# The first load of Q in a linear-attention kernel: one queue or two

## The chip, the cores and the metric

The kernel runs on one core of a Trainium2 chip. The metric is the time of one execution in microseconds on the device. A profiled execution gives in addition the span from the first to the last instruction and what every engine and DMA queue did inside it.

## The reference

For each of 8 x 12 heads, with Q, K and V of 512 rows by 64 in FP32:

```
Q_feat = np.maximum(0, Q) + 1
K_feat = np.maximum(0, K) + 1
KV = np.einsum('bhkd,bhkv->bhdv', K_feat, V)
K_sum = np.sum(K_feat, axis=2)
numerator = np.einsum('bhqd,bhdv->bhqv', Q_feat, KV)
denominator = np.einsum('bhqd,bhd->bhq', Q_feat, K_sum)
return (numerator / (denominator[:, :, :, None] + 1e-10)).astype(np.float32)
```

There is little arithmetic for each byte: 37.75 MB are read and 12.58 MB are written.

## The kernel before

The 96 heads are worked in 12 groups of 8 heads (`NG` is 12). Two neighbouring groups share their transfers: one load of K, one of V and one of Q, 1 MB each as it is written on chip, bring a pair of groups. These loads go by POOL's queue (`nc.gpsimd.dma_start`) and change FP32 to BF16 on the way, so each reads 2 MB from memory. The stores of all but the last two groups go by POOL's queue as well; the last ones go by SP's.

For one group, VectorE makes the features of K (`k_features`), VectorE and ScalarE copy V into a block layout (`v_blocks`: three copies of 32 partitions at L164 on VectorE, one at L162 on ScalarE), TensorE multiplies them (`keys_values`, L180), and ScalarE takes the result out of PSUM. VectorE makes the features of Q (`q_features`, L146), TensorE transposes them (L201), ScalarE copies the transposed tiles (L204), TensorE multiplies them by KV (`out_matmuls`, L214), and VectorE divides (`norms`, L231 and L232) into the tile that is stored.

The order of the work is written out by hand, under `tc.manual_schedule()`: each engine runs its instructions in the order of the program. The start matters here. The first pair of groups isn't loaded by three large loads: K and V come in two loads each, one per group, and Q comes in two halves of another kind. The first half is `q_first`, a tile of its own, loaded by `load_first_q` without a change of type, 128 rows of 8 KB, one for each partition; the second is loaded by `load_rest_q` on POOL's queue. In order of the program:

```
nc.gpsimd.memset(zero, 0.0)
q_first = load_first_q()
load("k", (0,))
load("v", (0,))
load_rest_q(q_first)
load("k", (1,))
load("v", (1,))
...
clear(0)
```

`clear` fills the block layout of V with zeros: VectorE takes five eighths (L249), ScalarE the rest (L250), then VectorE sets the columns of ones (L251). `q_first` is first read by `q_features(0)`, after the K features and V blocks of group 0.

Of the kernel before, what the change touches and what calls it, by code (L numbers as in the profile page):

```python
# [19 lines left out]
def kernel(  # L20
# [19 lines left out]
    nc = tc.nc  # L40

    B, H, S, D = Q.shape
    P = 128
# [10 lines left out]
    def view(t, c):  # L54
        return t.flatten_outer_dims().rearrange("(n p c) d -> p n c d", p=P, c=c)

    q_eights = view(Q, C4)
# [32 lines left out]

    def load_first_q():
        t = head_pool.tile([P, C4, D], FP32, name="q_first")
        nc.sync.dma_start(out=t, in_=q_eights[:, 0])
        return t

    def load_rest_q(t):
# [159 lines left out]
    with tc.manual_schedule():  # L256
# [4 lines that stand above are left out]
# [81 lines left out]
```

## Time and profile before

| | us |
|---|---|
| Time, median of 3 runs (lowest to highest) | 126.62 (126.32 to 127.39) |
| The profiled execution's own time | 126.47 |
| Its span, first to last instruction | 124.7 |
| VectorE busy | 90.1 |
| TensorE matmul busy | 64.2 |
| ScalarE busy | 59.6 |
| POOL busy | 26.1 |
| `q_first`: issue on SP, and from there to landing | 0.74, then 4.9 |

The busy times are inside the span. In the lines of the profile, PE is TensorE, DVE is VectorE, ACT is ScalarE, POOL is GpSimd and SP is SyncE. L93 and the like are lines of the kernel. In the slices, one digit is a fortieth of the span in tenths, so 9 is 90% or more. The DMA share is the time of the packets over the time of 16 DMA engines; packets overlap a little, so it can be above 1. The bytes are those written: a load that changes FP32 to BF16 counts half of what it reads. q0 is the queue that POOL feeds; q1 is a hardware queue, before the change that of SP. In a table of windows, the columns are the window, its length, the busy time and number of instructions of PE, PEld (weight loads), DVE, ACT and POOL, then the granted clock, the DMA share and GB/s.

### The profile page before, as it was taken

To read this page: it belongs to the slowest core of one execution; us is meant where nothing else is said; L and a number is where in the kernel's file an instruction comes from. 1 tells how busy PE (TensorE), PEld (TensorE's weight loads), DVE (VectorE), ACT (ScalarE), POOL (GpSimd) and SP (SyncE) were. 2 spreads that over 40 slices of the span, in tenths; PEclk is the share of its full clock that TensorE was granted. 3 is DMA by queue.
4 is the path that set the end of the run, shared out by engine and by line. 5 is a ranking of instruction groups with operands and counts; after the bars stand their busy time and mean duration, and the time that the engine had idled before them with its cause. 6 is when DMAs were issued, how large, how long until landed. Compare 5 with 4: busy or idle time off the path is not lost.

```text
span 124.7 us, 2349 instructions
## 1 busy us (share of the span) xinstructions
PE 64.2 (52%) x960; PEld 52.6 (42%) x960; DVE 90.1 (72%) x190; ACT 59.6 (48%) x86; POOL 26.1 (21%) x53
## 2 busy tenths in 40 slices
PE   0000874600596837939099690069394369874200
PEld 0000654600475826829088490058183158663000
DVE  4875735206999989998999950799958799969700
ACT  7505169806009981398803981603982283650000
POOL 6992020400001460207202070302020200020000
PEclk9999999995559996799855999657999855999655
DMA  3999999999999999999999999999999999999993
GB/s 89 320 212 216 206 211 212 212 215 218 206 212 212 220 213 206 212 215 217 230 406 327 210 212 219 212 342 395 230 202 215 219 247 417 419 417 415 406 409 135
DMA packets 11819, 32.13 MB, mean 258 GB/s; under 512 B 544, under 2 KB 544, under 8 KB 11680
## 3 DMA queue, kind: packets, MB, share of 16 engines
q0 software_dynamic: 10592, 28.84, 97.5%
q1 hardware_dynamic: 1216, 3.15, 6.7%
q8 instruction: 7, 0.11, 0.3%
q14 instruction: 4, 0.03, 0.1%
HBM read 37.75 MB, written 12.58 MB: 404 GB/s over the span
## 4 chain that ended last, share of the span: by engine, by line
DMA 51%; DVE 19%; PE 10%; ACT 7%; POOL 6%; issue 2%; DVEq 0%; ACTq 0%; POOLq 0%
DMA v_raw<-in_V_dram 51%; DVE o_sb L232 7%; PE kva_ps L180 7%; DVE v_all L164 7%; ACT qt L204 3%; ACT v_all L162 3%; POOL kva_all L271 2%; POOL k_raw L115 2%; DVE recip L231 2%; PE qt_ps L201 1%; PE o_ps L214 1%; POOL v_raw L115 1%; DVE qf L146 1%; DVE qt L204 1%; DVE kf L146 1%
## 5 line engine op out<-in xcount | busy, mean ns | idle before, releaser
L180 PE MATMUL kva_ps<-v_all,kf 128*64 128x260 bf16 x384 | 33.0, 343 | 16.8 <-DVE v_all L164 15.5
L214 PE MATMUL o_ps<-kva_all,qt 128*64 128x130 bf16 x384 | 19.7, 237 | 34.2 <-DVE recip L231 25.9
L164 DVE COPY v_all<-v_raw 32x2048 bf16<-32x2048 bf16 x36 | 26.1, 725 | 15.0 <-DMA v_raw<-in_V_dram 14.6
L180 PEld LDWEIGHTS <-kf 128*64 128x64 bf16 x384 | 26.6, 140 | 20.4 <-DVE v_all L164 15.9
L232 DVE TENSOR_TENSOR o_sb<-o_ps,recip 128x512 f32<-128x512 f32 x48 | 33.2, 692 | 1.6
L162 ACT COPY v_all<-v_raw 32x2048 bf16<-32x2048 bf16 x12 | 22.6, 1893 | 18.2 <-DMA v_raw<-in_V_dram 18.0
L214 PEld LDWEIGHTS <-qt 128*64 128x64 bf16 x384 | 13.7, 116 | 39.1 <-issue 23.2
L190 ACT CAST kva_all<-kva_ps 64x256 bf16<-64x256 f32 x24 | 8.9, 370 | 30.7 <-PE kva_ps L180 30.6
L204 ACT COPY qt<-qt_ps 128x1024 bf16<-128x1024 bf16 x23 | 22.2, 1015 | 2.2 <-PE qt_ps L201 1.7
L201 PE MATMUL qt_ps<-identity,qf 128*128 128x128 bf16 x192 | 14.8, 236 | 1.3 <-ACT qt L204 1.1
L135 POOL DMA_DIRECT2D out_dram<-o_sb x10 | 8.3, 830 | 32.1 <-DVE o_sb L232 27.3
L146 DVE TENSOR_SCALAR kf<-k_raw 128x1024 bf16<-128x1024 bf16 x24 | 9.5, 436 | 7.0 <-DMA k_raw<-in_K_dram 7.0
L201 PEld LDWEIGHTS <-qf 128*128 128x128 bf16 x192 | 12.6, 107 | 4.1 <-issue 1.8
L115 POOL DMA_DIRECT2D k_raw<-in_K_dram x7 | 5.4, 765 | 34.4 <-DVE kf L146 34.0
L231 DVE RECIPROCAL recip<-o_ps 128x8 f32<-128x8 f32 x48 | 9.6, 200 | 1.5 <-PE o_ps L214 1.2
L115 POOL DMA_DIRECT2D v_raw<-in_V_dram x7 | 5.4, 772 | 17.4 <-ACT v_all L162 17.4
L146 DVE TENSOR_SCALAR qf<-q_raw 128x1024 bf16<-128x1024 bf16 x22 | 8.2, 432 | 0.0
L249 DVE MEMSET v_all<- 128x2600 f32 x2 | 4.5, 2225 | 1.1 <-issue 1.1
L191 ACT CAST kva_all<-kva_ps 64x4 bf16<-64x4 f32 x24 | 4.1, 169 | 0.0
L121 POOL DMA_DIRECT2D q_raw<-in_Q_dram x5 | 3.5, 705 | 0.0
L250 ACT COPY v_all<-zero 128x1560 f32<-128x1560 f32 x2 | 2.9, 1488 | 0.0
L271 POOL MEMSET kva_all<- 128x130 bf16 x16 | 2.4, 196 | 0.0
(14 smaller groups left out, 6.6 us busy)
## 6 DMA issues: line engine op xcount, KB each, us to landing
out_dram<-o_sb POOLq DMA_DIRECT2D x10, 1024.0 KB, 25.2
k_raw<-in_K_dram POOLq DMA_DIRECT2D x5, 1024.0 KB, 21.7
v_raw<-in_V_dram POOLq DMA_DIRECT2D x5, 1024.0 KB, 21.8
q_raw<-in_Q_dram POOLq DMA_DIRECT2D x5, 1024.0 KB, 25.9
q_first<-in_Q_dram SPq DMA_DIRECT2D x1, 1024.0 KB, 4.9
k_raw<-in_K_dram POOLq DMA_DIRECT2D x2, 512.0 KB, 9.7
v_raw<-in_V_dram POOLq DMA_DIRECT2D x2, 512.0 KB, 11.4
out_dram<-o_sb SPq DMA_DIRECT2D x1, 1024.0 KB, 7.0
```

The lines of the kernel that those rows point to most:

```text
L115: nc.gpsimd.dma_start(out=bufs[x, s][:, ms], in_=drams[x][:, of])
L135: nc.gpsimd.dma_start(out=o_to[:, g % 2 : 2 * NP : 2], in_=outs[s][:, g % 2 : 2 * NP : 2])
L146: nc.vector.tensor_scalar(out=dst, in0=src, scalar1=1.0, scalar2=1.0, op0=ALU.add, op1=ALU.max)
L162: nc.scalar.copy(out=v_all[ps, g % 2, :, :, b * D : b * D + D], in_=v_raw[ps])
L164: nc.vector.tensor_copy(out=v_all[ps, g % 2, :, :, b * D : b * D + D], in_=v_raw[ps])
L180: nc.tensor.matmul(kva_ps[64 * n : 64 * n + 64], lhsT=kf[:, c, n, :], rhs=v_all[:, g % 2, n, c, :], start=(c == 0), stop=(c == C2 - 1),)
L190: nc.scalar.copy(out=kva[ps, :, n, 0:D], in_=kva_ps[ps, 0 : 4 * D].rearrange("p (b d) -> p b d", b=4))
L201: nc.tensor.transpose(qt_ps[:, c, r], qf[:, r, 2 * half + c, :, :], identity)
L204: copy(out=qts[g // 2][:, lo : lo + 2], in_=qt_ps.rearrange("p c r q -> p c q r"))
L214: nc.tensor.matmul(ops[c // 4][64 * j : 64 * j + 64, c // 2 % 2, (c % 2) * W : (c % 2) * W + W], lhsT=qt[:, c, q : q + 16, :], rhs=kva[:, ...
L231: nc.vector.reciprocal(out=recip, in_=cells[:, :, :, :, D:D1])
L232: nc.vector.tensor_tensor(out=o_sb[:, 2 * h + g % 2 : 2 * NP : NP, 4 * i : 4 * i + 4].rearrange("p n (b c) d -> p b c n d", b=2), in0=cell ...
```

## The change

The first load of Q is issued as two transfers of 64 partitions each. The first goes by SP's queue, the second by ScalarE's. Where they stand in the program, the tile that they fill and all that reads it stay.

```
     def load_first_q():
         t = head_pool.tile([P, C4, D], FP32, name="q_first")
-        nc.sync.dma_start(out=t, in_=q_eights[:, 0])
+        nc.sync.dma_start(out=t[0 : P // 2], in_=q_eights[0 : P // 2, 0])
+        nc.scalar.dma_start(out=t[P // 2 : P], in_=q_eights[P // 2 : P, 0])
         return t
```

## The prediction, made before the change was run

> **What bounds the kernel now.** I began with the page: the slices (part 2) and the chain that ended last (part 4).
>
> ```profile
> span 124.7 us, 2349 instructions
> PE 64.2 (52%) x960; PEld 52.6 (42%) x960; DVE 90.1 (72%) x190; ACT 59.6 (48%) x86; POOL 26.1 (21%) x53
> DMA  3999999999999999999999999999999999999993
> HBM read 37.75 MB, written 12.58 MB: 404 GB/s over the span
> DMA 51%; DVE 19%; PE 10%; ACT 7%; POOL 6%; issue 2%; DVEq 0%; ACTq 0%; POOLq 0%
> ```
>
> No compute engine is above 72%, but the 16 DMA engines are full in every slice except the first and the last. The kernel is one long transfer of 50.3 MB with the arithmetic beside it. So the end is set by the time at which the DMA engines begin, by how fast they work, and by nothing that a compute engine does inside the slack that it has. A microsecond of DMA-engine time lost anywhere comes out at the end.
>
> Next I read the table of half-microsecond windows over the start. Its last two columns are the DMA share and GB/s.
>
> ```profile
> 1.50:2.00 0.50, 0.00 (x0) 0.00 (x0) 0.13 (x1) 0.50 (x1) 0.50 (x1) 1.00 1.13 131
> 2.00:2.50 0.50, 0.00 (x0) 0.00 (x0) 0.50 (x1) 0.49 (x2) 0.50 (x2) 1.00 0.00 0
> 2.50:3.00 0.50, 0.00 (x0) 0.00 (x0) 0.50 (x1) 0.50 (x1) 0.50 (x2) 1.00 0.68 279
> 3.00:3.50 0.50, 0.00 (x0) 0.00 (x0) 0.50 (x1) 0.50 (x2) 0.50 (x2) 1.00 0.97 410
> 4.50:5.00 0.50, 0.00 (x0) 0.00 (x0) 0.11 (x1) 0.41 (x1) 0.50 (x2) 1.00 1.17 483
> 5.00:5.50 0.50, 0.00 (x0) 0.00 (x0) 0.50 (x1) 0.00 (x0) 0.43 (x3) 1.00 1.06 168
> ```
>
> Packets are booked in the window in which they start. Eight start just before 2 us (one for each of eight engines), none in the next window, and from about 2.6 us all engines work: up to 5 us over 400 GB/s are written, which is plain FP32, the first Q; from 5 us about 200 GB/s, which is a casting load (4 bytes read for 2 written). The DMA queues of three windows say whose packets these are. First 3.0 to 3.5, then 4.5 to 5.0, then 5.0 to 5.5:
>
> ```profile
> q1 hardware_dynamic: 25, 0.20, 96.5%
> ...
> q1 hardware_dynamic: 31, 0.24, 112.2%
> q0 software_dynamic: 2, 0.00, 4.3%
> ...
> q0 software_dynamic: 41, 0.08, 104.2%
> q1 hardware_dynamic: 14, 0.00, 1.6%
> ```
>
> q1 is the hardware queue (the first Q), q0 is POOL's. They do not mix: K(0), issued on POOL at 1.29, moves nothing until an engine has done its share of Q. Therefore the first Q's transfer is fully exposed. It is the head of the kernel's one resource, even though VectorE needs its data much later.
>
> The timeline of the start shows that slack.
>
> ```profile
> 0.74 0.39 SPq L93 DMA_DIRECT2D q_first<-in_Q_dram  x1
> 2.03 2.88 ACT L250 COPY v_all<-zero 128x1560 f32<-128x1560 f32 x2
> 10.89 1.89 ACT L162 COPY v_all<-v_raw 32x2048 bf16<-32x2048 bf16 x1 [5.97 <-DMA v_raw<-in_V_dram]
> 12.95 0.69 DVE L146 TENSOR_SCALAR qf<-q_first 128x1024 bf16<-128x1024 f32 x1
> ```
>
> **The change part by part.** The sum is against the profiled execution: 126.47 us, a span of 124.7 and 1.77 around it. It lies 0.15 under the median of 126.62, which the forecast leaves aside.
>
> Issue on ScalarE (added): one DMA instruction, 0.39 us by SP's row. Behind it in ScalarE's program stand the two zero-fills of L250 and then the V copy of L162. ScalarE is idle for 5.97 us before 10.89, so 0.39, or even the 1.28 us of a table load with it, is covered. Without that cover 0.39 would delay V's blocks, and so TensorE, at 12.98. There is one nearer reader: VectorE's L251 at 4.20 writes over what ScalarE clears. ScalarE's first fill ends near 3.5 (2.03 plus 1.49), so 0.7 us are free there, and VectorE has 1.74 us idle before 10.81 after that. Cost 0.
>
> Issue on SP (halved): SP has nothing else until 114.28. Cost 0.
>
> Waits: VectorE's first reading of Q at 12.95 now needs two arrivals. Q landed at 5.64 (0.74 plus 4.9). Even 3 us later it is 4 us early. A second semaphore is worth an issue gap, 0.02 to 0.04 us in the chain, and VectorE idles 0.87 us before 15.79: cost 0. At the end the program also waits for ScalarE's queue, long done: 0 to 0.04, taken 0.
>
> Transfer of Q: bytes and packets stay. From the 3.0 to 3.5 row a packet takes 0.965 x 16 x 0.5 / 25 = 0.309 us. There are 128 rows of 8 KB, so 8 packets or 2.47 us on each engine. What the change alters is that each half covers only 64 partitions. No transfer in this trace does that (all loads and stores cover 128), so I bound it. The lower bound is no loss: the 0.309 us stay, 4 and 4 packets. The upper bound is that half the partitions take half the rate, 0.618 us a packet, so the two halves, drained one after the other as q1 and q0 were, cost 4.94 in place of 2.47: plus 2.47 us. I choose between them by what the rows suggest about the 0.309. It is 26.5 GB/s for one engine, and hardly moves from window to window; stores and casting loads give 25 and 24 GB/s on their wider side (16 engines at 417 and at 2 x 212, over 16 and with their overlap). That is a fixed width somewhere, at the engine or at the memory it writes. If at the memory, sixteen engines on half of it share it two by two. The row nearest in kind is that of Q itself: a transfer that writes 4 bytes an element at that width, so nothing is spare to hide the sharing. I take sharing, with one correction: the engines do not start together. The rows show two batches, at 1.84 (0.74 of issue plus 1.1) and at 2.62, 0.78 apart for 64 rows each. With 32 rows in a batch I expect 0.39. For that long at each end of a half, one of a pair has the width alone: 4 packets then take 0.39 + (4 - 0.39/0.309) x 0.618 = 2.08 for the first, and as much from its own start for the other. Two halves are 4.16, a loss of 1.7 us.
>
> The Trainium skill speaks against the change here: "SBUF — State Buffer", in the sections "Door 1: The DMA port swizzle" and "Can I just issue two DMAs to hit both halves?", says that partitions 0 to 63 reach only 8 of 16 ports, gives 196 GB/s for a 1 MiB load to them against 328 to all, and says that two concurrent halves gain about 6% on one. By its 6% on 196 GB/s, 1.05 MB would take an estimated 5.0 us, a loss of 2.6; nothing in this trace shows such a port.
>
> Start of Q (moved): data flows from about 2.6, when the second batch of engines starts. If half the rows on each queue bring that forward to the first batch, 0.78 us is gained; that is the lower end, minus 0.78. Against it: the eight early packets start before 2.0, and yet nothing follows in 2.0 to 2.5, so early descriptors alone did not bring early data. The upper end is 0, or later for one half if ScalarE loads its table first, which costs nothing while SP's half or K keeps the engines busy. I take minus 0.2.
>
> The skill's page "DMA: Bandwidth & Descriptors", section "Queues, rings and completion order", has an engine take turns between queues packet by packet; the rows above show q1 done before q0 starts. By turns, a pair could step to opposite halves after one packet, and the loss would go towards 0.
>
> Order of arrival: V(0), which VectorE and ScalarE wait for at 10.8, stands behind K(0) in POOL's queue and behind all of Q on the engines, so it is late by the loss. What is late next is every load and store behind it. POOL issued loads 20 us ahead of their landing (21.7 us from issue to landing in the page), so no queue runs empty, and the shift reaches the end whole.
>
> Sum: 126.47 + 1.7 - 0.2 = 128.0 us.
>
> **The rivals.**
>
> First, no sharing: the width belongs to the engine, or an engine alternates halves. Then only the start counts: 126.47 - 0.2 = 126.3, down to 125.7 if the whole 0.78 is gained. For it: the fixed 0.309 could as well be the engine's, and the DMA share is already above 1 with 16 engines. Against: all those rows spread over all partitions. This is the case on the other side, not slower; it decides if a half's packet stays below about 0.34 us (8 x 0.03 is 0.2).
>
> Second, partial sharing: ScalarE's half comes after its table load (1.28 us), the engines are out of step, and some run K while their partner is on Q. Half of the loss is left: 126.47 + 0.85 - 0.2 = 127.1. For it: the table load stands at 0.74 in ScalarE's program now, and K is ready by then. Against: partners tend to meet again in the second half.
>
> Third, the split does not do what it says: the second half is drained strictly after the first, at full rate, or waits behind K and V. Q would land near 11 and still before 12.95: 126.5. I count it with the first.
>
> **How the numbers follow.** Sharing 0.52, partial 0.18, none (with the third) 0.30. The forecast is the likeliest, 128.0; its own range runs from 127.2 (more gained at the start) to 128.8 (126.47 + 2.47 less a little). A tenth of the cases lies above 128.7; the lowest tenth, a third of the no-loss case, lies below about 126.0. The range is 126.0 to 128.7. One per cent of the median, 1.27 us, is about what can be told from no change: sharing gives more than that in some eight of ten of its cases, partial in one of ten: slower 0.44. Faster by so much would need more than the 0.78 at the start: 0.04. Within 1%: 0.52.
>
> **What would show it.** Right: windows from 2.5 to 7 us with about 200 to 280 GB/s written by the hardware queues, packets near 0.6 us, K's first packet at 6.5 or later, V's landing 1.5 us after its 10.8, and the same tail shifted. Wrong: over 400 GB/s until 5 us (no sharing), K starting before 4.6 (a gain at the start), VectorE idle at 12.95 waiting for Q (the order broke), or a shift at 10.8 that is gone by 98.8, when the last V lands (the DMA was not the limit throughout).

## The result, and the profile after

The changed kernel takes 128.24 us (median of 6 runs, 127.87 to 128.74), against 126.59 (126.32 to 127.39, 6 runs) for the kernel before in the same comparison: a ratio of 1.0117, with an interval of 1.0093 to 1.0140. It is slower by 1.65 us. The profiled execution took 128.13 us, its span 126.4 (before: 126.47 and 124.7).

The page of the kernel after: the span, the DMA slices, the memory line, and the chain by engine.

```profile
span 126.4 us, 2351 instructions
...
DMA  3999999999999999999999999999999999999993
...
HBM read 37.75 MB, written 12.58 MB: 398 GB/s over the span
...
DMA 52%; DVE 18%; PE 9%; ACT 6%; POOL 5%; issue 2%; DVEq 0%; POOLq 0%
```

The DMA engines are as full as before and move the same bytes, but at 398 GB/s over the span instead of 404. So some stretch of full engines moved less. The table of half-microsecond windows of the kernel after shows which (the last two columns are the DMA share and GB/s):

```profile
2.00:2.50 0.50, 0.00 (x0) 0.00 (x0) 0.50 (x1) 0.50 (x1) 0.50 (x2) 1.00 1.42 262
2.50:3.00 0.50, 0.00 (x0) 0.00 (x0) 0.50 (x1) 0.49 (x2) 0.50 (x2) 1.00 0.67 262
3.00:3.50 0.50, 0.00 (x0) 0.00 (x0) 0.50 (x1) 0.50 (x1) 0.50 (x2) 1.00 1.14 262
3.50:4.00 0.50, 0.00 (x0) 0.00 (x0) 0.50 (x1) 0.50 (x1) 0.50 (x1) 1.00 1.30 262
...
4.50:5.00 0.50, 0.00 (x0) 0.00 (x0) 0.12 (x1) 0.50 (x1) 0.50 (x2) 1.00 0.84 197
...
6.00:6.50 0.50, 0.00 (x0) 0.00 (x0) 0.50 (x1) 0.00 (x0) 0.50 (x5) 1.00 1.30 262
6.50:7.00 0.50, 0.00 (x0) 0.00 (x0) 0.50 (x1) 0.00 (x0) 0.50 (x4) 1.00 0.56 98
```

Before, the first Q was written at over 400 GB/s until 5 us. Now it is written at 180 to 262 GB/s, and it lasts until 6.5 to 7. The DMA queues of the kernel after, in the windows 3.5 to 4, 4 to 4.5 and 6.5 to 7, say whose packets these are. q1 is SP's queue, q10 ScalarE's, q0 POOL's; the columns are packets, MB, and their time as a share of the 16 engines.

```profile
q1 hardware_dynamic: 16, 0.13, 129.7%
...
q10 hardware_dynamic: 11, 0.09, 87.1%
q1 hardware_dynamic: 11, 0.00, 2.6%
...
q0 software_dynamic: 24, 0.05, 52.0%
q10 hardware_dynamic: 15, 0.00, 3.6%
```

A packet of SP's half in the first of these windows takes 1.297 x 16 x 0.5 / 16 = 0.65 us, against 0.309 before. On an engine, ScalarE's half starts only when SP's is done (the 11 packets of 0.00 MB hold 4 bytes each and follow SP's last packet there), and K only when ScalarE's is done.

The records of the single packets, counted from the start of the span like the timeline, show more than the windows. The four packets of SP's half on an engine take 0.71, 0.33, 0.57 and 0.65 us on the mean of the 16 engines, the four of ScalarE's half 0.62, 0.55, 0.62 and 0.65. Before, the first took 0.73 and the seven others 0.31 to 0.32. The first is long in both kernels; the slow pace begins with the third. The first 16 packets of K start at 6.82 us on the mean, against 5.12 before: 1.69 us later. In what follows, "K starts" is this mean.

The first V blocks in the timeline of the kernel before:

```profile
10.81 2.11 DVE L164 COPY v_all<-v_raw 32x2048 bf16<-32x2048 bf16 x3 [1.74 <-DMA v_raw<-in_V_dram]
```

The timeline of the kernel after, from its start:

```profile
0.74 0.54 SPq L93 DMA_DIRECT2D q_first<-in_Q_dram  x1
0.74 0.56 ACTq L94 DMA_DIRECT2D q_first<-in_Q_dram  x1
...
1.33 1.28 ACT L251 ACT_TABLE_LOAD   x1 [1.33 <-PEq L327]
...
2.63 2.88 ACT L251 COPY v_all<-zero 128x1560 f32<-128x1560 f32 x2
...
12.40 2.11 DVE L165 COPY v_all<-v_raw 32x2048 bf16<-32x2048 bf16 x3 [1.79 <-DMA v_raw<-in_V_dram]
...
14.55 0.69 DVE L147 TENSOR_SCALAR qf<-q_first 128x1024 bf16<-128x1024 f32 x1
```

The first V blocks move from 10.81 to 12.40, 1.59 later. Q is not waited for: its two halves land 4.8 and 7.1 us after their issue, so by 7.84, and are first read at 14.55. At the other end, SP issues the last stores in the kernel before

```profile
114.28 0.39 SPq L138 DMA_DIRECT2D out_dram<-o_sb  x1
...
115.96 2.05 SPq L141 DMA_DIRECT2D out_dram<-o_sb  x2
```

and in the kernel after

```profile
115.89 0.39 SPq L139 DMA_DIRECT2D out_dram<-o_sb  x1
...
117.57 2.05 SPq L142 DMA_DIRECT2D out_dram<-o_sb  x2
```

which is 1.61 later. What is lost in the first 7 us is there at 12 us, at 115 and at the end, and nothing is added on the way.

### The profile page after: what moved, and what is told of

Its sections match the earlier page's. It is cut to its first block, busy times and chain, and to the rows that moved or that the text cites. A ratio compares the mean times of both kernels' runs of the same rounds, so it can differ in the third digit from the quotient of the medians.

```text
span 126.4 us, 2351 instructions
## 1 busy us (share of the span) xinstructions
PE 65.6 (52%) x960; PEld 53.5 (42%) x960; DVE 90.2 (71%) x190; ACT 59.6 (47%) x86; POOL 26.1 (21%) x53
## 4 chain that ended last, share of the span: by engine, by line
DMA 52%; DVE 18%; PE 9%; ACT 6%; POOL 5%; issue 2%; DVEq 0%; POOLq 0%
DMA v_raw<-in_V_dram 52%; DVE o_sb L233 7%; DVE v_all L165 7%; PE kva_ps L181 6%; ACT qt L205 3%; ACT v_all L163 3%; PE qt_ps L202 2%; POOL kva_all L272 2%; POOL k_raw L116 2%; DVE recip L232 2%; POOL v_raw L116 1%; DVE qf L147 1%; PE o_ps L215 1%; DVE qt L205 1%; DVE kf L147 1%
## 5 line engine op out<-in xcount | busy, mean ns | idle before, releaser
L215 PE MATMUL o_ps<-kva_all,qt 128*64 128x130 bf16 x384 | 20.3, 242 | 32.9 <-DVE recip L232 24.5
L215 PEld LDWEIGHTS <-qt 128*64 128x64 bf16 x384 | 14.2, 119 | 38.0 <-issue 20.6
L202 PE MATMUL qt_ps<-identity,qf 128*128 128x128 bf16 x192 | 15.3, 240 | 1.5 <-ACT qt L205 1.4
L251 ACT COPY v_all<-zero 128x1560 f32<-128x1560 f32 x2 | 2.9, 1488 | 0.0
```

The lines of the kernel that those rows point to most:

```text
L202: nc.tensor.transpose(qt_ps[:, c, r], qf[:, r, 2 * half + c, :, :], identity)
L215: nc.tensor.matmul(ops[c // 4][64 * j : 64 * j + 64, c // 2 % 2, (c % 2) * W : (c % 2) * W + W], lhsT=qt[:, c, q : q + 16, :], rhs=kva[:, ...
```

## The experiments

The theory: 64 partitions in one stretch (0 to 63, or 64 to 127) take data at half the rate, so two such halves one after the other cost the exposed head twice its time. The rival: the second queue, or two queues at once, costs the time. A third question is whether it is the number of partitions that matters, or which ones.

**Both halves on one queue.** ScalarE issues nothing.

```
+        nc.sync.dma_start(out=t[0 : P // 2], in_=q_eights[0 : P // 2, 0])
+        nc.sync.dma_start(out=t[P // 2 : P], in_=q_eights[P // 2 : P, 0])
```

Expected: 

> Both halves (partitions 0 to 63, then 64 to 127) go by SP's queue, one after the other; ScalarE issues nothing. Sharing theory (64 partitions carry only half the rate, whichever queue): the packets of Q stay near 0.6 us, K starts near 6.5 us, and the time is that of the change, about 128.2 (ratio to before 1.010 to 1.015). Rival, two queues (the cost comes from the second queue, ScalarE's, and its hand-over): packets of 0.31 us, K at 5.2, about 126.6 (ratio 0.998 to 1.002).

Measured: 128.11 us, ratio 1.0109 (1.0073 to 1.0145). Its DMA queues from 3.5 to 4 us:

```profile
q1 hardware_dynamic: 16, 0.13, 129.5%
```

Again 0.65 us a packet, and K starts at 6.77. The loss is whole without a second queue.

**The whole load on the other queue.**

```
+        nc.scalar.dma_start(out=t, in_=q_eights[:, 0])
```

Expected: 

> The whole first Q, undivided, by ScalarE's queue. Sharing theory: packets of 0.31 us and 126.5 to 126.8 (ratio 0.999 to 1.002). Two-queue theory, in the form that ScalarE's queue is slow: over 127.5.

Measured: 126.58 us, ratio 0.9986 (0.9965 to 1.0007). From 3 to 3.5 us ScalarE's queue shows

```profile
q10 hardware_dynamic: 23, 0.19, 90.8%
```

which is 0.908 x 8 / 23 = 0.316 us a packet; K starts at 5.05. ScalarE's queue costs nothing that could be told here, nor does its table load behind the issue.

**Even and odd partitions.** This keeps all of the change, two queues and 64 partitions each, and alters only which partitions stand together.

```
+        nc.sync.dma_start(out=t[0:P:2], in_=q_eights[0:P:2, 0])
+        nc.scalar.dma_start(out=t[1:P:2], in_=q_eights[1:P:2, 0])
```

Expected: 

> Two queues, 64 partitions each, but SP takes the even partitions and ScalarE the odd ones, so that each half is spread over the whole memory. If only the set of partitions in a transfer counts (the low 64 or the high 64 share, spread ones don't): packets of 0.31 us, K starts at 5.2, about 126.6 (ratio 0.998 to 1.003). If it counts which partitions the sixteen engines write at one moment (an engine's four rows lie eight partitions apart from its neighbour's, so two engines still meet): packets near 0.6 us and about 128.2.

Measured: 126.90 us, ratio 1.0006 (0.9978 to 1.0034). Its DMA queues from 4 to 4.5 us:

```profile
q10 hardware_dynamic: 23, 0.19, 91.1%
q1 hardware_dynamic: 13, 0.01, 5.2%
```

0.911 x 8 / 23 = 0.317 us a packet on ScalarE's queue; K starts at 5.30. The loss is gone. Of the two forms written down beforehand, the first held: what counts is which partitions a transfer holds. The second, that engines would still meet row by row, did not; which rows an engine takes is not in the records, so what that form assumed of them is not tested.

**Half the load: the low 64 partitions, or the middle 64.** In these two kernels the rest of the first Q is left out and set to zero by POOL, so both move half of its bytes.

```
+        nc.sync.dma_start(out=t[0:64], in_=q_eights[0:64, 0])      # one kernel
+        nc.sync.dma_start(out=t[32:96], in_=q_eights[32:96, 0])    # the other
```

Expected, low: 

> Only partitions 0 to 63 of the first Q are loaded (SP's queue); the rest is left out and set to zero by POOL. Half of the bytes. Sharing theory: half the bytes at half the rate take as long as the whole did, so about 126.4 (no gain; with the earlier start perhaps 126.1). Without sharing: 4 packets of 0.31 us fewer on each engine, 126.6 - 1.24 = 125.4.

Expected, middle: 

> Only partitions 32 to 95 are loaded, the rest left out and set to zero. If it is which partitions: full rate, packets of 0.31 us, 125.4 or, with the earlier start, 125.0. If it is the number of partitions: as with partitions 0 to 63, 126.1 to 126.4.

The DMA queue from 3.5 to 4 us with the low half,

```profile
q1 hardware_dynamic: 14, 0.11, 113.6%
```

and with the middle half:

```profile
q1 hardware_dynamic: 29, 0.24, 112.0%
```

1.136 x 8 / 14 = 0.65 us a packet against 1.12 x 8 / 29 = 0.309. The number of partitions and the queue are the same, and the rate differs by two. One thing these runs leave open: in every kernel here the 8 KB row p of this load goes to partition p, so they don't tell whether the slow side is the memory written or the memory read.

The middle half took 125.83 us, ratio 0.9933 (0.9911 to 0.9955): 0.84 less than before, where 1.24 was expected, since its first data came later (first 8 KB done at 3.15 us, before at 2.76) and K started 0.96 earlier, not 1.24. With the low half K started 0.63 earlier, where nothing was expected: as in the change, an engine's second packet still took 0.33 us. The low half took 127.15, ratio 0.9985 (0.9942 to 1.0028). Its time settles nothing: four runs lie at 125.69 to 126.05, six at 127.10 to 127.64. The last section tells what the profile of one of the upper six shows. Besides, VectorE's work is longer beside POOL's zeroing (three V copies take 5.41 us with the middle half, 2.11 before), so the rates say more here than the times.

**The middle and two quarters.**

```
+        nc.sync.dma_start(out=t[32:96], in_=q_eights[32:96, 0])
+        nc.scalar.dma_start(out=t[0:32], in_=q_eights[0:32, 0])
+        nc.scalar.dma_start(out=t[96:128], in_=q_eights[96:128, 0])
```

Expected: 

> SP loads partitions 32 to 95 (64 of them), ScalarE's queue 0 to 31 and then 96 to 127 (32 each). If it is the number of partitions that counts, all three run at half rate or less and the time is 128.2 or above. If it is which partitions (0 to 63 share their paths, and so do 64 to 127, but 32 to 63 and 64 to 95 don't), the first transfer runs at the full rate and the other two at half: half of the loss, about 127.3 (ratio 1.004 to 1.008).

Measured: 126.97 us, ratio 1.0018 (0.9994 to 1.0042), less than either form of the theory gave. K starts at 5.11, as before. The packet records suggest why: the first quarter went out ahead of the middle, and its first 8 KB were done from 2.19 us on, 0.6 earlier than with the undivided load. This made up for what was slow later: the middle's first packets took 0.51 to 0.65 us, its second 0.31 to 0.52, and the last quarter's second ones 0.48 to 0.61.

That suggested both quarters first, as a version that might beat both kernels:

```
+        nc.sync.dma_start(out=t[0:32], in_=q_eights[0:32, 0])
+        nc.scalar.dma_start(out=t[96:128], in_=q_eights[96:128, 0])
+        nc.sync.dma_start(out=t[32:96], in_=q_eights[32:96, 0])
```

Expected: 

> SP loads partitions 0 to 31 and ScalarE's queue 96 to 127 first (32 each), then SP loads 32 to 95. Sharing theory: the first two pieces run at half rate while the engines are waiting for data anyhow, the middle runs at the full rate, K starts near 5.0: 126.3 to 126.6 (ratio 0.997 to 1.000). If the number of partitions or the second queue cost something of their own: 127 or more.

Measured: 127.03 us, ratio 1.0031 (1.0002 to 1.0059), a miss. K starts at 5.36. The middle's first packets took 0.47 to 0.51 us and its second 0.36 to 0.51, not the 0.31 of the middle half alone. Quarters still under way on other engines can't be the whole reason, since their last packet was done at 4.14 and several of these packets started later; the rest is open. By its time alone the run fits the second form (127 or more), but the number of partitions and the second queue cost nothing of the kind in the kernels above. No division tried here beats the undivided load.

**Halves by columns.** Two queues, every transfer on all 128 partitions, 4 KB of each.

```
+        nc.sync.dma_start(out=t[:, 0 : C4 // 2], in_=q_eights[:, 0, 0 : C4 // 2])
+        nc.scalar.dma_start(out=t[:, C4 // 2 : C4], in_=q_eights[:, 0, C4 // 2 : C4])
```

Expected: 

> Two queues as in the change, but the halves are columns: each transfer writes all 128 partitions, 4 KB of each. Sharing theory: full rate, over 400 GB/s while Q is loaded, packets of 4 KB near 0.16 us, and only the start counts: 126.2 to 126.7 (ratio 0.995 to 1.001). Two-queue theory: about 128.2, as with the change (ratio 1.010 or more).

Measured: 126.93 us, ratio 1.0018 (0.9990 to 1.0045): not the loss of the change, but no gain either, and a little above the 126.2 to 126.7 expected. Its DMA queues from 3.5 to 4 us:

```profile
q10 hardware_dynamic: 25, 0.10, 50.0%
q1 hardware_dynamic: 25, 0.10, 49.9%
```

Full rate, 0.16 us for 4 KB, and here the engines take turns between the queues.

**Half of the columns only.** The other half of the first Q is left out and set to zero.

```
+        nc.sync.dma_start(out=t[:, 0 : C4 // 2], in_=q_eights[:, 0, 0 : C4 // 2])
```

Expected: 

> Only the first half of the columns is loaded, on all 128 partitions; the rest is left out and set to zero. Both theories: full rate and 1.24 us less of the DMA engines' time, 125.4. It measures whether DMA time saved at the head reaches the end whole: if it does, ratio about 0.990; if the rest of the kernel has slack, nearer 1.

Measured: 126.75 us, ratio 0.9996 (0.9967 to 1.0026), 1.35 above the expected 125.4. K starts at 4.37, 0.75 earlier than before, but its features start at 9.02, where before they start at 8.31. Something else took the time back; see the last section.

**The whole load twice.** This asks directly what a lost microsecond at the head costs.

```
         nc.sync.dma_start(out=t, in_=q_eights[:, 0])
+        u = head_pool.tile([P, C4, D], FP32, name="q_again")
+        nc.sync.dma_start(out=u, in_=q_eights[:, 0])
```

Expected: 

> The whole first Q on SP's queue as before, and then the same bytes again into a tile that nothing reads: 8 more packets of 0.31 us on every engine ahead of K. If DMA time lost at the head reaches the end whole, as the explanation needs: plus 2.5 us, 129.1 (ratio 1.017 to 1.022). If the rest of the kernel takes part of it up: 127.5 to 128.5.

Measured: 129.16 us, ratio 1.0178 (1.0129 to 1.0227), 2.57 above the median of before for 8 x 0.309 = 2.47 us of packets. The first V blocks:

```profile
13.25 2.11 DVE L166 COPY v_all<-v_raw 32x2048 bf16<-32x2048 bf16 x3 [1.79 <-DMA v_raw<-in_V_dram]
```

2.44 later than before. DMA time added at the head reaches the end whole. In one point the run differs from what was expected: the second copy didn't go ahead of K. K's first packets start at 5.70 us and go between the copy's, whose last is done at 8.83; the packets to be moved before V are the same.

## Why the prediction was right, and where it was not

It gave 128.0 us; the profiled execution took 128.13 and the median is 128.24.

*The bound.* "A microsecond of DMA-engine time lost anywhere comes out at the end" was shown for time added at the head, by the load made twice and by the shift of the change itself: 1.69 at K's start, 1.59 at V, 1.61 at the last stores, 1.7 in the span. For time saved at the head it was shown only in part: with the middle half K started 0.96 earlier and the time fell by 0.84, with half of the columns K started 0.75 earlier and the end did not move.

*The issue on ScalarE.* It took 0.56 us, not the 0.39 of SP's row, and pushed the table load and the first fill back by 0.6, to an end near 4.1. The 0.7 us named as free before L251 were just enough: L252 of the new kernel (the old L251) stands at 4.20 as before. The cover held, but it was nearly used up. SP's issue, which the prediction called halved, grew from 0.39 to 0.54 us, at no cost.

*The waits.* Two arrivals in place of one cost nothing, as said. Q was there 6.7 us before VectorE read it.

*The transfer.* The term of plus 1.7 rested on a choice between two bounds. The choice was right: from the third packet of an engine on, a packet takes 0.61 us on the mean (0.618 was assumed), both halves meet it, and they follow each other. But no row of before decided it, and the prediction gave it a chance of only 0.52. The correction from 2.47 to 1.7 came out in size and not by its reason, which is luck. It let an engine have the width alone for 0.39 us at each end of a half, and so took as much off each half. In the run all 16 engines start within 0.31 us, the second packets of SP's half are the ones that stay near the full pace (0.33), and none of ScalarE's is below 0.52. ScalarE's half lost about 1.2 us (2.44 for its four packets, 1.24 at the full pace), SP's about 0.6. Why the second packets are fast is not known.

From the first packet to the end of the last, Q takes 4.98 us (2.07 to 7.05), 210 GB/s for 1.05 MB; before it took 3.51 (1.76 to 5.27). What the rows of before could not show is now shown: engines, rows and queue do not set the pace alone, since the same 16 engines with the same number of rows take 0.309 us a packet to partitions 32 to 95, or to every second one, and 0.60 and 0.65, in the third and the fourth packet, to 0 to 63. Whether the 0.309 itself belongs to the engine or to the memory stays open.

The Trainium skill's page "SBUF — State Buffer", section "Door 1: The DMA port swizzle", agrees with the pace: it gives partitions 0 to 63 half of the ports, and 196 GB/s. The prediction's estimate of 5.0 us from that page is what Q took, but its "loss of 2.6" set a whole transfer against the 2.47 us of packets alone; whole against whole, 4.98 to 3.51, it is 1.5. The section "Can I just issue two DMAs to hit both halves?" says that only one transfer over all 128 partitions reaches them all. The runs show no ports, but by the pace the measurement decides against that sentence: partitions 32 to 95 alone, and even and odd ones in two transfers, keep the full pace.

*The start.* Minus 0.2 was wrong: the gain was nothing. All 16 engines start between 2.07 and 2.38, where before eight started at 1.76 to 1.84, and the first 8 KB are done at 2.84 (before at 2.76). The argument given against a gain, that early descriptors did not bring early data, held for the whole of it.

*The order.* "K's first packet at 6.5 or later" and "V's landing 1.5 us after its 10.8" came out at 6.7 and 1.59. The rival without sharing fell with its own sign: the windows no longer show 400 GB/s. The rival of partial sharing fell too: ScalarE's table load came after its issue, and apart from the last 0.3 us no engine was at K while another was at Q.

So the sum was right with 1.7 and 0 where 1.7 and minus 0.2 were written, and the 0.13 us to the profiled time lie in that second term. That sharing would cost the time was right as a mechanism; that the first term met its size so closely was partly luck.

## What to carry to other kernels

When the DMA engines are full from end to end, look for what they do alone and unhidden at the head, and price a change by the engines' time for it and not by when its data are needed. A load over half of the partitions is not half a load: divided into 0 to 63 and 64 to 127 it lost 1.65 us, by even and odd partitions nothing that could be told. A second queue neither cost nor brought anything that could be told here.

## What the runs showed that was not expected

A transfer of 64 partitions takes its issuing engine longer than one of 128: 0.53 to 0.60 us in all the kernels with such a transfer, against 0.38 to 0.42 for one that covers all 128, on SP and on ScalarE alike.

Whether a DMA engine drains one queue before it turns to another, or takes turns, differed: with the low and high halves and with even and odd ones it drained SP's transfer first; with columns it took turns packet by packet, and K's packets went between those of the second copy of Q. What decides was not found.

An earlier K does not always arrive earlier. In the profiled execution with half of the columns, K's casting load ran slowly for a microsecond or more just after its start, with full engines. Windows of a microsecond from 5 us on, first the kernel before and then half of the columns:

```profile
5.00:6.00 1.00, 0.00 (x0) 0.00 (x0) 1.00 (x1) 0.00 (x0) 0.93 (x7) 1.00 1.02 176
6.00:7.00 1.00, 0.00 (x0) 0.00 (x0) 1.00 (x1) 0.00 (x0) 1.00 (x8) 1.00 1.11 209
```

```profile
5.00:6.00 1.00, 0.00 (x0) 0.00 (x0) 1.00 (x1) 0.00 (x0) 0.93 (x7) 1.00 0.95 139
6.00:7.00 1.00, 0.00 (x0) 0.00 (x0) 1.00 (x1) 0.00 (x0) 1.00 (x8) 1.00 1.10 188
```

The packet records show single packets of 0.4 to 0.9 us there instead of 0.17; with the low half alone two of 1.5 and 1.7 us near 5.4 us, after which those two engines were behind, and they ended the kernel at 124.6 where the other fourteen were done by 123.3. This fits the two groups of that kernel's times, which lie about 1.5 us apart. The profiled execution with halves by columns, at 127.74 us the second longest of its kernel, has four such packets of 1.2 to 1.3 us. The middle half, whose K started earliest of all (4.17), had none above 0.34 in the first 12 us. The cause stays open.
